# A hybrid encoder layer on one Trainium2 core: w_out's sums, the first pair's operands and half of Norm 2 get new places

## The chip, the core and the metric

The kernel runs on one core of a Trainium2 chip. The core has a matrix engine (TensorE, here PE, with its weight loads PEld), a vector engine (VectorE, DVE), a scalar engine for activations (ScalarE, ACT), a general engine (GpSimd, POOL) and SyncE (SP), which here issues all DMAs. Each works through its own instructions in order and waits on semaphores for the others. Matmuls read the on-chip memory SBUF and write PSUM banks; DVE and ACT empty these. The metric is the device time of one execution in microseconds (us); lower is better.

## The reference

One layer over 2048 rows of width 1024, in fp32. Cut to what matters:

```python
mod  = silu(c) @ w_mod + b_mod                    # 6 vectors: shifts, scales, gates
h    = rms_norm(x, g_norm1) * (1 + scale1) + shift1
qa, ka, va, qm, km, vm, om, gates = split(h @ w_in)
att  = banded_attention(qa, ka, va, sink)         # 8 heads, |t - s| <= 128
mls  = mlstm(conv(qm), conv(km), vm, gates, forward) + mlstm(..., backward)
mix  = concat(rms_norm(att) * g_attn, rms_norm(mls) * g_mlstm * sigmoid(om))
x1   = x + gate1 * (mix @ w_out)
h2   = rms_norm(x1, g_norm2) * (1 + scale2) + shift2
x2   = x1 + gate2 * ((silu(h2 @ w_g) * (h2 @ w_u)) @ w_ffn_out)
out  = rms_norm(x2, g_final)
```

## The kernel before

**Products.** Every fp32 operand is split into a high part (rounded by ACT) and a low part (the rest, by DVE), and one product is three matmuls: high by high, high by low, low by high (`mm3`, L56 to L58). The large products also use a Strassen-like scheme with 7 instead of 8 sub-products on 2 x 2 blocks, for which sums of blocks are formed first.

**Stages**, by the profile's time: up to 192 us modulation, Norm 1 and first projections; to 622 the conv tiles and the mLSTM of four heads, each a reverse pass and a forward pass over 16 chunks of 128 rows; to about 845 attention in 32 units; to 885 the last output gates (`o_tiles`); to 1108 the out projection in eight pairs of row tiles; then the FFN. PE's order is written by hand from the conv stage on: generators in a list `fill` yield one matmul each and `pull(n)` takes n of them in between other work. For the other engines a scheduler sets the order up to the out projection; from `rest` on (L1045) DVE, ACT, POOL and SP work in the order in which the code issues them, until `rest.close()`.

**mLSTM.** For a chunk POOL makes `ng` (L585, decay and mask) and `qs` (L590, scaled queries) from `bc` and `mqk`, which SP loads; ACT takes the exponential of `ng`; PE makes scores `sps`; DVE multiplies them to `sc` (L594); PE adds up `num`. `mv` holds values, `vw` and `kvp` belong to the state.

**w_out's sums.** `w_out_ops` (L855 on) multiplies w_out by the gate and forms the sub-products' seven right operands, on POOL, and stores them to `wo_d`. One group is a block of columns and a k: two loads (`bx`, `by`), multiplications (L871), four differences (L875), seven stores. It advances by `next(wops)` in attention, behind whose units POOL also scales the probabilities `ap` (L695). `start_wo(u)` loads operand u back, `finish_wo(u)` splits it (L892, L893).

**Out projection.** `Pair(p)` loads two tiles of attention's output twice (`msq` to square, `ma` to use), the mLSTM's output `mm` and the output gate `og`. Then: ACT squares, POOL adds (L978, L979), PE sums over partitions (`aps`), DVE takes the root (`rsqrt`) and builds two diagonals, PE spreads them (`arb`), DVE scales (L995) and gates (L998), POOL makes the sums (L1011 to L1020), ACT and DVE split them (L1006, L1007) into the seven left operands. `out_proj` (L1026) runs seven units u of 4 k x 3 matmuls into three PSUM banks. After a unit DVE adds its bank to the rows `xr` of x (L1038), and after units 5 and 6 the rows, now x1, are stored. The loop takes one of 28 steps of a pair with each `pull(1)`, and the next pair's work at fixed steps.

**Norm 2.** `norm2(hh, z, ...)` handles a block of 512 rows: four loads of x1 (`x1t`, L1091), squares (L1100), root, scaling (L1106), PE transposes, ACT's affine (`n`, L163), and for the second block of a half the FFN's sums with the first block's operands, read back from `hop_d`; all operands go to `hop_d`. `refill_ops` loads them (`T`, `B`) and splits them; a FFN unit is `pair(hh, j, ...)`, whose first product is emptied by ACT to `s` (L1302). While pairs 2 and on run, `norm2(0, ...)` is taken a piece every second step; the first FFN unit runs beside pieces of `norm2(1, ...)`.

## Time and profile before

| | us |
|---|---|
| three timed runs, median | 2423.81 |
| lowest and highest | 2422.14, 2426.52 |
| the profiled execution | 2431.26 |
| its span, first to last instruction | 2429.5 |
| PE busy in it | 2271.0 |
| DVE, ACT, POOL busy | 1579.1, 1060.9, 1029.5 |

The profiled execution has its own time, above the timed runs' highest. In the views, each row of instructions names the line, the engine, the operation and the tiles (out <- in); a row of waits names the waiting instruction, then what released it, with the total, the number of times and the longest. "ops" is the PSUM bank of the out projection, "fp" that of a FFN unit, "gps" that of a projection.

### The profile page before, as it was taken

The page shows a single profiled execution, that of the slowest core. Times are in us where ns is not written, and L with a number is a line of the kernel's source. Part 1 is how long each engine was busy: PE and PEld are TensorE (multiplying, and loading weights), DVE is VectorE, ACT ScalarE, POOL GpSimd, SP SyncE. Part 2 cuts the span into 40 slices and gives each one's busy share as a digit, 9 for nine tenths or more (in the row PEclk, how much of TensorE's full clock was granted, in tenths as well). Part 3 has the DMA queues.
Part 4 walks back from the last instruction along what each step waited for, and adds up shares of the span by engine and source line. Part 5 has one row for each costly group of instructions (what it writes and reads, how often), then busy time and mean ns, then how long its engine had stood idle before and what let it go on. Part 6 is the DMA issues. An engine that isn't in the chain of part 4 may idle for free.

```text
span 2429.5 us, 32711 instructions
## 1 busy us (share of the span) xinstructions
PE 2271.0 (93%) x10801; PEld 1876.6 (77%) x10801; DVE 1579.1 (65%) x3096; ACT 1060.9 (44%) x2133; POOL 1029.5 (42%) x874
## 2 busy tenths in 40 slices
PE   5988999999999968888999999999999999999998
PEld 4987777788777856766887887788888888778886
DVE  6774677657677756558655776766566536684584
ACT  4523455544676733426444444543444323223352
POOL 1001234334466333253655565456556546483020
PEclk9999999999999989989999999999999999999999
DMA  7674455576878566685353453533333264453452
GB/s 288 173 239 104 134 164 159 165 214 173 234 239 248 156 212 199 224 282 209 104 169 105 145 178 94 208 91 105 108 111 106 87 212 149 134 173 95 135 200 91
DMA packets 363522, 401.86 MB, mean 165 GB/s; under 512 B 24670, under 2 KB 255576, under 8 KB 363352
## 3 DMA queue, kind: packets, MB, share of 16 engines
q1 hardware_dynamic: 363352, 399.78, 52.0%
q8 instruction: 85, 1.39, 0.2%
q14 instruction: 85, 0.70, 0.1%
HBM read 280.50 MB, written 119.19 MB: 165 GB/s over the span
## 4 chain that ended last, share of the span: by engine, by line
PE 52%; DVE 5%; DMA 4%; issue 2%; ACT 1%; POOL 1%; SPq 1%; DVEq 0%; ACTq 0%; POOLq 0%
PE fp L56 11%; PE fp L58 11%; PE fp L57 11%; PE fo L58 5%; PE fo L57 5%; PE fo L56 5%; PE ops L56 1%; PE ops L57 1%; PE ops L58 1%; DMA hop_d<-n 1%; DMA x1t<-x_d 1%; DMA al<-a_d 1%; PE gps L417 1%; SPq L965 0%; DVE wo L893 0%
## 5 line engine op out<-in xcount | busy, mean ns | idle before, releaser
L417 PE MATMUL gps<-hT,whi 128*128 128x512 f32 x1088 | 400.0, 423 | 12.4 <-ACT ctanh L431 7.3
L56 PE MATMUL fo<-w,ah 128*128 128x512 f32 x616 | 242.6, 394 | 3.0 <-ACT ah L1384 2.9
L58 PE MATMUL fo<-w,al 128*128 128x512 f32 x616 | 243.2, 395 | 1.8 <-DVE al L1385 1.8
L57 PE MATMUL fo<-w,ah 128*128 128x512 f32 x616 | 243.2, 395 | 0.0
L417 PEld LDWEIGHTS gps<-hT,whi 128*128 128x128 f32 x1088 | 203.8, 193 | 38.7 <-ACT ctanh L431 7.7
L417 PE MATMUL gps<-hT,wlo 128*128 128x512 f32 x544 | 229.8, 422 | 0.0
L56 PE MATMUL fp<-T,S 128*128 128x512 f32 x528 | 209.7, 397 | 15.1 <-ACT s L1302 12.5
L58 PE MATMUL fp<-T,S 128*128 128x512 f32 x528 | 208.2, 394 | 0.0
L57 PE MATMUL fp<-T,S 128*128 128x512 f32 x528 | 208.1, 394 | 0.0
L1385 DVE TENSOR_TENSOR al<-al,ah 128x1024 fp32r<-128x1024 f32 x77 | 114.0, 1485 | 137.3 <-ACT ah L1384 137.1
L1186 DVE TENSOR_TENSOR A<-graw,A 128x512 fp32r<-128x512 f32 x86 | 106.3, 1256 | 119.0 <-ACT A L1185 119.0
L1384 ACT ACTIVATE ah<-al 128x1024 fp32r<-128x1024 f32 x77 | 81.7, 1061 | 199.7 <-DMA al<-a_d 197.8
L56 PEld LDWEIGHTS fo<-w,ah 128*128 128x128 f32 x616 | 116.1, 188 | 31.4 <-ACT ah L1384 3.8
L58 PEld LDWEIGHTS fo<-w,al 128*128 128x128 f32 x616 | 115.8, 188 | 29.9 <-DVE al L1385 3.5
L58 PE MATMUL fp<-B,A 128*128 128x512 f32 x352 | 137.6, 391 | 0.0
L56 PE MATMUL fp<-B,A 128*128 128x512 f32 x352 | 137.6, 391 | 0.0
L57 PE MATMUL fp<-B,A 128*128 128x512 f32 x352 | 137.6, 391 | 0.0
L57 PEld LDWEIGHTS fo<-w,ah 128*128 128x128 f32 x616 | 116.0, 188 | 26.7
L56 PEld LDWEIGHTS fp<-T,S 128*128 128x128 f32 x528 | 100.2, 190 | 38.3 <-ACT s L1302 13.4
L1186 DVE TENSOR_TENSOR S<-sf,S 128x512 fp32r<-128x512 f32 x86 | 90.9, 1058 | 44.0 <-ACT S L1185 43.9
L58 PEld LDWEIGHTS fp<-T,S 128*128 128x128 f32 x528 | 99.9, 189 | 22.4
L57 PEld LDWEIGHTS fp<-T,S 128*128 128x128 f32 x528 | 100.2, 190 | 21.7
(376 smaller groups left out, 6067.5 us busy)
## 6 DMA issues: line engine op xcount, KB each, us to landing
al<-a_d SPq DMA_DIRECT2D x77, 512.0 KB, 3.5
wmod<-in_w_mod_dram SPq DMA_DIRECT2D x48, 512.0 KB, 5.8
graw<-in_w_ffn_in_dram SPq DMA_DIRECT2D x43, 512.0 KB, 4.6
a_d<-ka SPq DMA_DIRECT2D x66, 256.0 KB, 2.3
bc<-bc_d SPq DMA_DIRECT2D x64, 256.0 KB, 3.8
hop_d<-n SPq DMA_DIRECT2D x56, 256.0 KB, 4.7
a_d<-u SPq DMA_DIRECT2D x55, 256.0 KB, 3.0
mqk<-qk_d SPq DMA_DIRECT2D x48, 256.0 KB, 4.1
```

The lines of the kernel that those rows point to most:

```text
L56: pe.matmul(o, lh, rh, start=first, stop=False, skip_group_check=skip)
L57: pe.matmul(o, lh, rl, start=False, stop=False, skip_group_check=skip)
L58: pe.matmul(o, ll, rh, start=False, stop=last, skip_group_check=skip)
L417: pe.matmul(ps, w[i == 2][:, k, :], hT[n](i == 1, k), start=(k == 0 and i == 0), stop=(k == KT - 1 and i == 2))
L1186: dve.tensor_tensor(t[:, 1, :], f, t[:, 0, :].bitcast(F32), SUB)
L1384: act.activation(ah, al.bitcast(F32), AF.Copy)
L1385: dve.tensor_tensor(al, al.bitcast(F32), ah.bitcast(F32), SUB)
```

## The change

Five things change.

1. `w_out_ops` moves ahead of the conv and mLSTM loop and is advanced there. It now has four column blocks of 128 instead of two of 256: 16 groups, each with two multiplications of 2 x 128 columns and four differences of 128.
2. A class `Pair` with single steps replaces the old one. Pair 0 goes through its steps in attention (`first_pair`, advanced from unit 21 on) with the first two operands of `wo`.
3. In the loop over pairs, loads come three pairs ahead, attention's output is loaded once, high splits (HI) and low splits (LO) are separate steps, and `xr` has five buffers.
4. For the first half of T, Norm 2 is done from the rows `xr` on chip, pair by pair, by the class `Rows`; its root is taken together with the next pair's. Its 128x512 tiles `n2` have nine buffers. The second half keeps `norm2`, now all on DVE.
5. In the last pair and the first FFN unit, the other engines' order is written out (`then=first_unit`), and `rest` closes behind that unit. `norm2(1, ...)` starts in the second unit. Rings of buffers are turned.

POOL's order in head 0, where the reverse pass ends; `wlo` is the low part of a conv weight, `ng` and `qs` belong to the scan. Before:

```order
L585 TENSOR_TENSOR ng<-bc,maskb 128x256 x2
L231 TENSOR_TENSOR wlo<-wraw,whi 128x1024
L590 TENSOR_TENSOR qs<-mqk,bc 128x256 x2
L231 TENSOR_TENSOR wlo<-wraw,whi 128x1024
L585 TENSOR_TENSOR ng<-bc,maskb 128x256 x2
```

Now, the last two of the groups that stand between `ng` and `qs`:

```order
L832 TENSOR_TENSOR bx<-bx,gb 128x256
L836 TENSOR_TENSOR ts<-bx 128x128
L832 TENSOR_TENSOR by<-by,gb 128x256
L836 TENSOR_TENSOR ts<-by,bx 128x128
L836 TENSOR_TENSOR ts<-by,ts 128x128 x2
L234 TENSOR_TENSOR wlo<-wraw,whi 128x1024
L832 TENSOR_TENSOR bx<-bx,gb 128x256
L836 TENSOR_TENSOR ts<-bx 128x128
L597 TENSOR_TENSOR qs<-mqk,bc 128x256 x2
```

Five groups, and the start of a sixth, have come ahead of the first `qs`.

SP's order at the same place, where the third `mv` of the reverse pass and the first `mqk` of the forward pass are loaded. Before:

```order
L433 DMA qk_d<-cacc 128x512 x3
L503 DMA mv<-vaug_d 128x4x129
L508 DMA mqk<-qk_d 128x512
L522 DMA bc<-bc_d 128x512
L503 DMA mv<-vaug_d 128x4x129
```

Now, first where `mv` stands, then, four rows further, where `mqk` stands:

```order
L436 DMA qk_d<-cacc 128x512
L839 DMA wo_d<-bx 128x128
L510 DMA mv<-vaug_d 128x4x129
L839 DMA wo_d<-by 128x128 x2
L839 DMA wo_d<-ts 128x128
L840 DMA wo_d<-ts 128x3x128
L824 DMA gb<-gate_d 128x128 x2
```

```order
L839 DMA wo_d<-bx 128x128
L839 DMA wo_d<-by 128x128 x2
L839 DMA wo_d<-ts 128x128
L840 DMA wo_d<-ts 128x3x128
L828 DMA bx<-in_w_out_dram 128x2x128
L515 DMA mqk<-qk_d 128x512
L828 DMA by<-in_w_out_dram 128x2x128
```

`mv` now stands behind the fourth group's first store, `mqk` behind the fifth group's stores.

POOL's order at the end of pair 3 and the start of pair 4 (`n` are the `n2` tiles of Norm 2, `ms` and `mm` the pair's sums, `msq` the next pair's squares). Now:

```order
L971 TENSOR_TENSOR mm<-mm,ms_11258 128x512
L1200 TENSOR_TENSOR n_11391<-n_11373,n_11360 128x512
L1203 TENSOR_TENSOR n_11322<-n_11322,n_11320 128x512
L1200 TENSOR_TENSOR n_11434<-n_11412,n_11399 128x512
L1203 TENSOR_TENSOR n_11326<-n_11326,n_11324 128x512
L941 TENSOR_TENSOR msq<-msq 128x256
L942 TENSOR_TENSOR msq<-msq 128x128
L941 TENSOR_TENSOR msq<-msq 128x256
L942 TENSOR_TENSOR msq<-msq 128x128
```

The second L1200 writes the buffer of `n_11373` (B22 of the first half), so it waits for that tile's store. Before, the pairs had only this between them:

```order
L1011 TENSOR_TENSOR ma<-ma 128x512
L1012 TENSOR_TENSOR ms_10887<-mm,ma 128x512
L1017 TENSOR_TENSOR ma<-ms_10887,ma 128x512
L1020 TENSOR_TENSOR mm<-mm,ms_10887 128x512
L978 TENSOR_TENSOR msq<-msq 128x2x256
L979 TENSOR_TENSOR msq<-msq 128x2x128
```

The Norm 2 sums of the first half have come in ahead of the squares' sums.

The diff, cut to its core:

```diff
@@ ahead of the conv and mLSTM loop (before: in front of attention) @@
+    wqs = ExitStack()
+    wq = wqs.enter_context(tc.tile_pool(name="wq", bufs=1, side="left", reuse_waits="tile"))
+    def w_out_ops():
-        for c_ in range(2):
-            cs = slice(c_ * 256, (c_ + 1) * 256)
+        for c_ in range(4):
+            cs = slice(c_ * P, (c_ + 1) * P)
+            gb = cp.tile([P, 2, P], F32, tag="gn", name="gb", bufs=1)
...
             for k in range(4):
+                bx, by = (wq.tile([P, 2, P], F32, tag=t, name=t) for t in ("bx", "by"))
+                for t, k_ in ((bx, k), (by, k + 4)):
+                    sp.dma_start(t, w_out[k_ * P:(k_ + 1) * P].rearrange("p (m c) -> p m c", m=2)[:, :, cs])
+                yield True
+                ts = wp.tile([P, 4, P], F32, tag="oth", name="ts", bufs=1)
+                for t in (bx, by):
+                    pool.tensor_tensor(t, t, gb, MUL)
+                    yield True
...
+                for u, t in ((0, bx[:, 0, :]), (1, by[:, 0, :]), (5, by[:, 1, :]), (6, ts[:, 3, :])):
+                    sp.dma_start(wo_d[u, k][:, cs], t)
+                sp.dma_start(wo_d[2:5, k, :, cs].rearrange("u p c -> p u c"), ts[:, 0:3, :])
+                yield True
@@ conv and mLSTM loop @@
     for h in range(HM):
-        for g in convs[h]:
-            finish_fill(g)
+        i = 0
+        while any(f is g for f in fill for g in convs[h]):
+            pull(1)
+            i += 1
+            if i % 2 == 0:
+                next(wops, None)
         last = load_last(h)
-        pull(60)
+        for i in range(60):
+            pull(1)
+            if i % 2 == 0:
+                next(wops, None)
         mlstm(h, 3, 8, last)
@@ class Pair @@
+        def square(self, i, sq):
+            act.activation(sq, self.a[:, i], AF.Square)
+            pool.tensor_tensor(sq[:, 0:2], sq[:, 0:2], sq[:, 2:4], ADD)
+            pool.tensor_tensor(sq[:, 0], sq[:, 0], sq[:, 1], ADD)
...
+        def hi(self):
+            u = len(self.ops)
+            self.f = (self.a11, self.a12, self.s2, self.a11, self.a21, self.a12, self.a22)[u]
+            self.ops.append(mring_tile(("mA11", "mA12", "mS2", "mS1", "mS3", "mS4", "mA22")[u]))
+            act.activation(self.ops[u][:, 0, :], self.f, AF.Copy)
+        def lo(self):
+            t = self.ops[-1]
+            dve.tensor_tensor(t[:, 1, :], self.f, t[:, 0, :].bitcast(F32), SUB)
@@ attention @@
-            if s_ > 4:
-                next(wops, None)
-        if not wo and s_ > 31 and lasts[0] not in fill:
-            for u in range(2):
-                start_wo(u)
+        if s_ > 20:
+            next(chain0, None)
@@ class Rows @@
+        def turn(self, k):
+            t = self.new()
+            ps = bank("bd"[self.n % 2], "trn")
...
+            for j in range(4):
+                pe.transpose(ps[:, j * P:(j + 1) * P], self.xr[j % 2][:, (k + j // 2) * P:(k + j // 2 + 1) * P], ident)
+            for j in range(2):
+                act.activation(t[:, j * 256:j * 256 + 256], ps[:, j * 256:j * 256 + 256], AF.Identity,
+                               bias=mod[:, 3, k + j:k + j + 1], scale=gs2[:, k + j:k + j + 1])
+            return t
+        def step(self, i):
...
+            g = 2 * (i > 20)
+            if i in (17, 21):
+                self.b12 = self.turn(g)
+            if i in (18, 22):
+                self.b22 = self.turn(g + 4)
+            if i in (20, 24):
+                b11, b12, b22 = self.t[g], self.b12, self.b22
+                self.t3 = self.new()
+                pool.tensor_tensor(self.t3, b22, b12, SUB)
+                dve.tensor_tensor(b12, b12, b11, SUB)
+                dve.tensor_tensor(b11, b22, b12, SUB)
+                pool.tensor_tensor(self.t[g + 1], self.t[g + 1], b11, SUB)
+                self.done = [("B22", g, b22), ("T3", g, self.t3), ("T1", g, b12), ("T2", g, b11), ("T4", g, self.t[g + 1])]
+            if i in (23, 27):
+                for o in self.done:
+                    self.put(*o)
@@ loop over pairs @@
-    OPERANDS = (5, 7, 10, 13, 16, 19, 23)
-    FIRST = (1, 2, 5, 8, 10, 14, 18)
+    HI, LO = (5, 8, 10, 14, 16, 19, 22), (6, 9, 11, 15, 17, 20, 23)
+    FIRST = (1, 2, 5, 8, 16, 20, 24)
...
-        if p in (2, 4):
-            norms.append(norm2(0, p // 2 - 1, "bd", 3))
...
+            if i == 18:
+                nx3 = Pair(p + 3) if p + 3 < NPR else None
+                if nx3:
+                    nx3.load_a()
...
+                if i == 7:
+                    ps = bank("a", "aps")
+                    for j in range(2):
+                        columns(ps, j, sq[j])
+                if i == 8:
+                    parts = [(ps[:, :2], 2, 512)] + ([(prev.ssq, 2, D)] if prev else [])
+                    r = rsqrt(mx, parts, 2 * len(parts), None, f"ar{len(parts)}")
...
+                prev.step(i)
+            if p < 4 and i == 25:
+                rows = Rows(p, xr0)
+                rows.square(0)
@@ FFN @@
+        def first_unit(u):
+            nonlocal nxt_w
             if u < 3:
                 finish_op(u + 4)
+            for _ in range((0, 0, 1, 1, 2, 1, 2)[u]):
+                nxt_w = next(more_w)
...
+            elif n == 0:
+                more_w = weights(raw)
+                pair(hh, j, ws_, hop, then=first_unit)
+                rest.close()
+                raw = load_raw(wseq.popleft())
```

397 lines of the change are left out of this document (227 added, 170 removed).

## The prediction

> **What bounds the kernel now.** I read the page's head first, then busy time by stage, then what TensorE (PE) waited for, and last the engines behind those waits. The profiled execution took 2431.3 us (span 2429.5, and 1.8 around it); the median of the three timed runs is 2423.8, so 7.4 us or 0.3% less. I sum against 2431.3 and take the 7.4 off at the end.
>
> ```profile
> span 2429.5 us, 32711 instructions
> PE 2271.0 (93%) x10801; PEld 1876.6 (77%) x10801; DVE 1579.1 (65%) x3096; ACT 1060.9 (44%) x2133; POOL 1029.5 (42%) x874
> ```
>
> PE is busy 93% of the span, so time can only go where PE stands still or runs slowly. The table by stage says where (columns: PE, weight loads, DVE, ACT and POOL busy with instruction counts, the clock granted to PE, the DMA engines' share):
>
> ```profile
> 885.00:920.00 35.00, 23.30 (x91) 18.10 (x91) 31.68 (x46) 17.18 (x23) 10.54 (x6) 0.85 0.38 120
> 920.00:974.00 54.00, 43.69 (x190) 35.20 (x189) 33.17 (x80) 19.36 (x29) 18.68 (x12) 0.94 0.61 200
> 974.00:1029.00 55.00, 46.76 (x221) 38.21 (x219) 32.04 (x79) 24.29 (x37) 17.12 (x12) 0.94 0.70 230
> 1029.00:1088.00 59.00, 47.91 (x206) 38.53 (x205) 34.92 (x60) 16.42 (x25) 31.47 (x21) 0.88 0.83 280
> 1088.00:1108.00 20.00, 20.00 (x90) 16.41 (x89) 14.84 (x20) 12.69 (x17) 1.30 (x1) 1.00 0.94 352
> 1108.00:1139.00 31.00, 22.26 (x86) 17.67 (x85) 25.25 (x34) 20.78 (x31) 12.94 (x9) 0.83 0.49 165
> 1139.00:1400.00 261.00, 256.33 (x1135) 209.43 (x1134) 159.11 (x180) 114.78 (x194) 151.00 (x104) 0.99 0.40 129
> ```
>
> From 885 to 1139 us run the out projection (eight pairs of row tiles) and the first FFN unit: 254 us. Only the pair at 1088 runs without a break; elsewhere PE is idle for 15 to 33%, and the clock is reduced too. From 1139 on it is 2%. The rows give 884 matmuls; 9 x 84 = 756 of them are the 128x512 products, which start 0.23 us apart at full clock (below): 172 us. The other 128 are short, about 5 us by their number. So about 77 us of the 254 are lost. What PE waited for from 868 on (the fourth row is one wait in front of the stage, at 873):
>
> ```profile
> PE ops L56 <- DVE xr L1038: 29.7, 8, 7.8
> PE fp L56 <- ACT s L1302: 8.7, 1, 8.7
> PE trn L162 <- ACT n L163: 5.4, 2, 5.0
> PE gps L417 <- ACT oth L489: 5.1, 1, 5.1
> PE ops L56 <- ACT mA L1006: 4.8, 1, 4.8
> PE aps L985 <- POOL msq L979: 3.7, 2, 2.3
> ```
>
> (Columns: total, times, longest.) The five rows of the stage make 52 us, so about 25 of the 77 are slow clock and short pauses; with the 5.1 in front 82 are lost. A matmul of the next unit waits until VectorE (DVE) has emptied its PSUM bank, and DVE works in written order behind low-half splits that wait for ScalarE (ACT). ACT in turn:
>
> ```profile
> ACT n L163 <- DMA hop_d<-n: 26.8, 5, 11.7
> ACT junk L1100 <- DMA x1t<-x_d: 16.2, 2, 8.2
> DMA to landing us min/median/max: 7.1/7.7/8.3
> ```
>
> So Norm 2's reload of x1 (`x1t`; the third row is its landing, 7.7 us in the median) holds ACT, ACT holds DVE, DVE holds PE. A stall also costs something behind itself:
>
> ```profile
> 1073.18 0.79 PE L56 MATMUL ops<-wo,mS 128*128 128x512 f32 x1 [3.07 <-DVE xr L1038]
> 1073.77 0.63 PE L57 MATMUL ops<-wo,mS 128*128 128x512 f32 x1
> 1074.20 0.63 PE L58 MATMUL ops<-wo,mS 128*128 128x512 f32 x1
> ...
> 1076.88 0.40 PE L56 MATMUL ops<-wo,mS 128*128 128x512 f32 x1
> 1077.11 0.40 PE L57 MATMUL ops<-wo,mS 128*128 128x512 f32 x1
> ```
>
> After a wait of 3.07 us the matmuls start 0.43 us apart until about 1076.5, then 0.23: some 1.7 us more. The Trainium skill, TensorE: Matmul & The Clock Gate, section "HAM oscillation — how this bites in real kernels", gives the rule that PE must not idle for more than about 3.4 us; here 3.07 us were enough, and the measurement decides. By the page's limit the new waits below, which I put at 3.5 us, would be at its edge and the sum could be 3 us smaller; by the row they pay.
>
> **Part 1, out projection and first FFN unit: 82 us lost, 28 left, gain 54.** For the first half of T Norm 2 now squares the rows that are still on chip; eight x1t loads go, and with them the two ACT waits (16.2 us), and the hop reads in front of `n` come ten steps ahead of use. Operands are loaded three pairs ahead; high and low splits are separate steps, so DVE no longer stands behind a split that waits for ACT. Work per pair stays: DVE has 7 adds, 7 low splits, 4 scalings and a gate in each pair:
>
> ```profile
> L1038 DVE TENSOR_TENSOR xr<-xr,ops 128x512 f32<-128x512 f32 x56 | 38.1, 681 | 18.3 <-PE ops L58 18.3
> L1007 DVE TENSOR_TENSOR mA<-mm,mA 128x512 fp32r<-128x512 f32 x15 | 15.1, 1006 | 4.6 <-ACT mA L1006 4.6
> L995 DVE SCALAR_TENSOR_TENSOR ma<-ma,cols,arb 128x256 f32<-128x256 f32 x28 | 11.6, 474 | 5.4 <-PE arb L993 5.4
> L998 DVE SCALAR_TENSOR_TENSOR mm<-og,mm 128x1024 f32<-128x1024 f32 x7 | 8.5, 1216 | 0.0
> L1123 POOL TENSOR_TENSOR n<-n,n 128x512 f32<-128x512 f32 x4 | 5.1, 1286 | 5.3 <-DMA hop_d<-n 5.3
> ```
>
> 7 x 0.68 + 7 x 1.0 + 4 x 0.47 + 1.2 = 14.9 us, and some 3 for the root, against 19.3 us (84 x 0.23) of PE: it fits, so a pair's stalls can go. Two pairs get four sums of Norm 2 on DVE as well (no row shows them there; below the 1.29 of POOL's row each), up to 23: these two are tight. What I leave: 5 us of the entry into pair 0 (pair 0's operands now come out of attention, but the low splits of `wo` still stand in DVE's order), 6 in pairs 1 to 3, 4 in pairs 6 and 7, 3 in the first FFN unit, whose 8.7 us wait goes because no Norm 2 of the second block stands in it. Nothing measures these; bounds are 0 and 29: the 5.1, 4.8, 5.4 and 3.7 above, 19 us, with 1.7 of slow clock for each of the six.
>
> And one **new wait**, 10 us. Pairs 3 and 4 write five results per half and the nine `n2` buffers go round. POOL's second T3 writes the buffer of the first B22, whose store to hop_d is issued only behind unit 5's x1 store, and lands late:
>
> ```profile
> hop_d<-n SPq DMA_DIRECT2D x56, 256.0 KB, 4.7
> ```
>
> So POOL stands from step 24 to about 5 us later. Behind it on POOL: its 1.3 us, the T4 sum 1.3, then the next pair's sums of squares (2.4), which PE needs at step 7: 10.0 us of work in 11 steps x 0.68 = 7.5, some with DVE's sum in between, whose queue holds the PSUM adds. About 3.5 us of PE and 1.5 of slow clock, twice: 10. Bounds 0 (if the store lands in 2 us) and 20.
>
> **Part 2, attention: gain 7.** The 64 POOL instructions and the loads they wait for leave:
>
> ```profile
> L871 POOL TENSOR_TENSOR bx<-bx,gb 128x256 f32<-128x256 f32 x16 | 11.6, 736 | 25.9 <-DMA bx<-in_w_out_dram 25.6 <-DMA by<-in_w_out_dram 0.3
> PE atp L702 <- POOL ap L695: 8.6, 18, 3.4
> ```
>
> 64 x 0.74 = 47 us of POOL and 25.6 of waiting stood in `ap`'s queue, and PE waited 8.6 us for `ap`, one time long enough for the slow clock (some 2 us). Pair 0's loads, squares, root, scaling and gate come in instead, a few us over 13 steps: 10.6 less 3.6. Bounds 0 and 12.
>
> **Part 3, mLSTM: loss 16.** The same sums now come as 16 groups in 128-wide pieces beside the conv and the scans: 2 multiplications of 0.74 us and 4 differences at about 0.46 (an estimate: 0.74 for 256 wide and 1.29 for 512 differ by 0.55), 3.3 us a group. bx and by have one buffer each, so a cycle is: load (4.0, row below), 3.3, two stores to issue (0.8): about 8.1 us. In head 0's reverse pass five such cycles stand in POOL's and SP's order. SP reaches the load of the gate only after the store of the conv in the second row, and the mLSTM's own loads are queued behind the cycles:
>
> ```profile
> DMA to landing us min/median/max: 3.5/4.0/4.3
> 239.45 6.05 SPq L433 DMA_DIRECT2D qk_d<-cacc  x2
> 262.71 0.37 SPq L503 DMA_DIRECT2D mv<-vaug_d  x1
> 263.65 0.93 SPq L508 DMA_DIRECT2D mqk<-qk_d  x1
> 279.09 0.38 PE L592 MATMUL sps<-mqk 128*128 128x128 f32 x1 [1.61 <-DVE cb L565]
> ```
>
> The gate lands at about 243.5. The third `mv`, behind the fourth group's first store, is issued at 243.5 + 3 x 8.1 + 0.7 = 268.5 instead of 262.7; the forward pass's first `mqk`, behind the fifth group's stores, at 243.5 + 4 x 8.1 + 4.6 = 280.5 instead of 263.7, and it lands about 284.5. PE needs it at 279.1: 5.4, say 6 us. In the forward passes POOL's `ng` has a slack:
>
> ```profile
> 280.31 0.73 POOL L585 TENSOR_TENSOR ng<-bc,maskb 128x256 f32<-128x256 f32 x1 [3.20 <-DVE sc L594]
> 284.58 0.42 DVE L594 SCALAR_TENSOR_TENSOR sc<-sps,ng 128x256 f32<-128x256 f32 x1
> L104 DVE TENSOR_TENSOR mra<-mra,mrh x48: 148/161/2159, 298.7 to 608.2; 128x4 f32<-128x4 f32 x48
> ```
>
> from 281.0 to 284.6, less two ACT steps: about 2.7 us. A half group puts 1.2 to 2.1 us ahead of an `ng`, and up to 4 of waiting for a load. Seven groups, 14 halves, 0.7 us each beyond the slack: 10. Bounds of part 3: 0 (all within slack) and 14 x 2 + 12 = 40.
>
> **Sum:** -54 - 7 + 16 = -45; 2431.3 - 45 = 2386.3, and less 7.4: **2379 us**.
>
> **Rivals.** (a) *The entry and the new wait are hidden.* For it: in pair 1088 to 1108 PE shows no idle time though DVE was 74% busy. Then 10 + 5 + 3 us more go: 2361. (b) *The new wait runs on.* DVE's queue behind POOL makes the next pairs start late too, and five of them pay 7 us (the longest wait at `xr` is 7.8 now) in place of 10 in all: 25 us more, 2404. For it: DVE and POOL are coupled there now too (the 5.3 us in the T3 row), against it: pairs 5 to 7 store nothing to hop_d. (c) *The change doesn't do what it says:* the x1t loads go but the waits under "xr L1038" come from DVE's own order, so half of the 29.7 and of the 25 us of slow clock stays: 27 us back, 2406. Against it is the chain shown above. (d) *Slower: the mLSTM pays more than the rest gains.* POOL is one queue; if a group's whole 8.1 us cycle lies on PE's path, the gain of 61 is gone after 7.5 of the 16 groups, that is, once half of them land in the scans without slack; with nine it is 73: 2424 - 61 + 73 = 2436. For it: half of the groups do stand in the two heads' passes. Against it: only the part beyond 2.7 us counts. The `mra` row feeds it: a tiny DVE instruction of 0.16 us took 2.16 beside one of POOL's. The Trainium skill, GPSIMD Engine Reference, section "1. Specifications", says that POOL's SBUF interfaces are shared with VectorE and that instructions with two SBUF inputs contend; the trace agrees with that 2.16 us. By that rule each of the 96 instructions could hold DVE for its own length, at most 53 us on top.
>
> **How the numbers follow.** Forecast as summed 0.56; (a) 0.12; (b) 0.13; (c) 0.08; (d) 0.07; and 0.04 for an mLSTM loss that just eats the gain. A measurement of this kernel tells about 0.2% (5 us) from no change. Faster: 0.89, within: 0.04, slower: 0.07. The range reaches from (a)'s with 10 us of the bounds, 2351, past (b) and (c) to 2412, and leaves out (d).
>
> **What would show it.** Right: no `x1t` in the first half, `ops <- xr` under 12 us, no wait over 3 us in the first FFN unit, and a wait at `aps` in the pairs behind 3 and 4 with POOL behind hop_d. The mLSTM's end moves from 622 to about 638 and its loads `mv` and `mqk` go out late. Wrong: if the mLSTM ends at 625 or at 660; if PE waits in pair 0 as before; or if POOL never stands for hop_d.

## The result, and the profile after

| | before | after |
|---|---|---|
| timed runs, median, us | 2423.14 (4 runs, 2422.14 to 2426.52) | 2407.76 (4 runs, 2406.51 to 2408.81) |
| ratio, with 95% interval | | 0.9934 [0.9917, 0.9951] |
| profiled execution, us | 2431.26 | 2408.62 |

The change makes the kernel 15.4 us faster between the medians, 0.66% by the ratio. The forecast was 2379: 28.8 us too low, inside its range of 2351 to 2412. Between the two profiled executions the gain is 22.6 us, where the sum said 45. The head of the page of after:

```profile
span 2406.8 us, 32761 instructions
PE 2275.5 (95%) x10801; PEld 1889.9 (79%) x10801; DVE 1587.8 (66%) x3078; ACT 1062.4 (44%) x2157; POOL 1032.1 (43%) x922
```

Both kernels have 10801 matmuls, and but for a stretch from 750 to 1066 us, in which short ones have moved, in the same order, so the k-th matmul of one can be set against the k-th of the other. (At 873 after has four products of the gates fewer behind it and four short matmuls more, about 0.9 us.) The table gives after's start less before's, worked out from the two traces: a falling number is time gained, a rising one time lost.

| matmul that starts in before at | shift, us | what lies between |
|---|---|---|
| 240 (first groups of w_out begin in after) | -2.7 | not touched by the change |
| 279 (first `sps` of head 0's forward pass) | +5.5 | reverse pass of head 0 |
| 300, 360, 400 | +11.2, +23.5, +30.2 | heads 0 and 1 |
| 622 (first attention score) | +32.7 | rest of head 1, heads 2 and 3: the mLSTM lost **35.4** in all |
| 873 | +18.4 | attention gained **14.3** |
| 1108 (first FFN unit starts) | -18.3 | entry and eight pairs gained **36.7** |
| 1139 (second unit starts) | -29.3 | first unit gained **11.0** |
| 1152 | -18.5 | second unit gave **10.8** back |
| 2400 | -22.5 | little |

So after is 4.0 us better in the FFN and 2.7 us ahead before the change begins. Both are of the size by which executions of one kernel differ (single runs of before on the chips lay between 2417.7 and 2431.3). The table by stage of after shows the same from PE's side (columns as in the prediction; stages cut where the same matmuls stand):

```profile
899.00:930.00 31.00, 23.47 (x90) 18.37 (x89) 28.62 (x45) 16.39 (x25) 9.72 (x8) 0.83 0.42 134
930.00:968.00 38.00, 38.00 (x188) 31.58 (x187) 30.27 (x65) 22.15 (x38) 17.58 (x16) 1.00 0.61 199
...
1090.00:1109.50 19.50, 19.15 (x84) 15.29 (x83) 18.53 (x17) 12.75 (x19) 7.91 (x4) 1.00 0.83 302
1109.50:1133.50 24.00, 17.29 (x58) 13.15 (x57) 18.11 (x30) 14.59 (x23) 11.93 (x8) 0.82 0.36 110
```

Pairs 1 and 2 (second row) and the first unit (third row) now run almost without a break; the entry (first row) keeps 7.5 us of idle time, and the pairs that the dots leave out keep 5.9. Behind the first unit stands a stretch that was not there in before: 24 us with PE idle for 6.7 of them and its clock at 0.82. What PE waited for from 870 to 1140, first, and the heaviest waits of the mLSTM stage of after, second (columns: total, times, longest):

```profile
PE aps L989 <- POOL msq L942: 10.8, 8, 2.7
PE fp L56 <- ACT u L1460: 4.6, 2, 4.2
PE ops L56 <- DVE xr L1090: 4.2, 2, 3.5
PE fp L56 <- ACT s L1452: 2.5, 1, 2.5
...
PE sps L599 <- DVE sc L601: 16.3, 9, 3.7
PE kvp L548 <- DVE den L629: 6.8, 2, 5.0
PE ktp L538 <- ACT og L648: 5.1, 1, 5.1
PE sps L599 <- DMA mqk<-qk_d: 4.8, 1, 4.8
```

The same view of before, from 240 to 622, has none of these long ones:

```profile
PE sps L592 <- DVE sc L594: 7.6, 8, 1.8
PE kvp L541 <- DVE den L622: 3.6, 2, 2.1
```

`xr` fell from 29.7 to 4.2, as forecast. In the mLSTM waits of 3.7 to 5.1 us are new. They are not the whole loss. The same matmuls as a stage, before and after:

```profile
240.00:622.00 382.00, 359.25 (x2021) 303.00 (x2019) 260.52 (x909) 183.82 (x563) 136.77 (x156) 0.99 0.59 169
```

```profile
237.50:654.70 417.20, 371.56 (x2020) 313.62 (x2019) 268.99 (x909) 182.87 (x563) 188.82 (x252) 0.95 0.64 184
```

Of the 35 us, 23 are idle time of PE (22.8 to 45.6), and 12 are its busy time, which grew while the granted clock fell from 0.99 to 0.95: the matmuls run slowly here too. SP's issues in head 0's reverse pass of after show where the first of them come from (start, duration, transfer):

```profile
266.56 0.43 SPq L510 DMA_DIRECT2D mv<-vaug_d  x1
...
277.56 0.42 SPq L840 DMA_DIRECT2D wo_d<-ts  x1
...
278.72 0.55 SPq L515 DMA_DIRECT2D mqk<-qk_d  x1
```

`mv` goes out at 266.6 (forecast 268.5, before 262.7), `mqk` at 278.7 (forecast 280.5, before 263.7): SP stands at w_out's stores until POOL has made their data. POOL in turn waits for the loads in front of them (busy, mean ns; then idle time in front and what ended it):

```profile
L832 POOL TENSOR_TENSOR bx<-bx,gb 128x256 f32<-128x256 f32 x16 | 12.4, 777 | 54.1 <-DMA bx<-in_w_out_dram 47.7 <-DMA gb<-gate_d 6.1 <-DMA bc<-bc_d 0.3
```

### The profile page after: what moved, and what is told of

The parts are those of the page before. It is cut to its first block, busy times and chain, and to the rows that moved or that the text cites. A ratio compares the mean times of both kernels' runs of the same rounds, so it can differ in the third digit from the quotient of the medians.

```text
span 2406.8 us, 32761 instructions
## 1 busy us (share of the span) xinstructions
PE 2275.5 (95%) x10801; PEld 1889.9 (79%) x10801; DVE 1587.8 (66%) x3078; ACT 1062.4 (44%) x2157; POOL 1032.1 (43%) x922
## 4 chain that ended last, share of the span: by engine, by line
PE 72%; DVE 8%; DMA 8%; issue 4%; POOL 3%; ACT 3%; SPq 1%; POOLq 0%; ACTq 0%; DVEq 0%
PE fp L56 11%; PE fp L57 11%; PE fp L58 11%; PE gps L420 8%; PE fo L58 6%; PE fo L56 6%; PE fo L57 5%; PE ops L56 2%; PE ops L57 2%; PE ops L58 2%; DMA bc<-bc_d 1%; PE atp L709 1%; DMA vst_d<-vs 1%; DVE macc L336 1%; PE as L686 1%
## 5 line engine op out<-in xcount | busy, mean ns | idle before, releaser
L420 PEld LDWEIGHTS gps<-hT,whi 128*128 128x128 f32 x1088 | 205.8, 195 | 30.8 <-ACT ctanh L434 5.0
L56 PEld LDWEIGHTS fp<-T,S 128*128 128x128 f32 x528 | 101.1, 191 | 37.3 <-ACT u L1460 8.2
L702 POOL TENSOR_SCALAR ap<-ap,adn 128x384 f32<-128x384 f32 (+1 forms) x128 | 72.9, 588 | 130.9 <-DVE adn L700 57.2
L58 PEld LDWEIGHTS fp<-T,S 128*128 128x128 f32 x528 | 101.0, 191 | 22.8
```

The lines of the kernel that those rows point to most:

```text
L56: pe.matmul(o, lh, rh, start=first, stop=False, skip_group_check=skip)
L58: pe.matmul(o, ll, rh, start=False, stop=last, skip_group_check=skip)
L420: pe.matmul(ps, w[i == 2][:, k, :], hT[n](i == 1, k), start=(k == 0 and i == 0), stop=(k == KT - 1 and i == 2))
L702: pool.tensor_scalar(self.p[g][:, :self.NK], self.p[g][:, :self.NK], dn[:, g:g + 1], 0.0, MUL, ADD)
```

## The experiments

In every run the mLSTM's loss is measured in one way: the shift against before at matmul 622 less that at 240. All times of single runs are one profiled execution. Up to the out projection POOL, VectorE and ACT have the same instructions in the same order in after, f_skip, f_step, f_pool and o_noput, so these five show how far one and the same code differs from execution to execution: the mLSTM lost 34.0 to 38.6 us in them, and attention gained 9.7 to 15.2. A difference under 5 us between two runs of the table shows nothing.

| run | shift at 240 | at 622 | mLSTM lost | time, us |
|---|---|---|---|---|
| after | -2.7 | +32.7 | 35.4 | 2408.6 |
| m_none | +6.7 | +7.4 | 0.7 | 2384.9 |
| m_nopool | +3.7 | +8.4 | 4.7 | 2387.3 |
| m_noload | -1.8 | +19.6 | 21.4 | 2397.9 |
| m_spread | +1.3 | +38.6 | 37.3 | 2411.7 (median) |
| m_poolq | -3.7 | +73.3 | 77.0 | 2449.2 |
| m_db | -0.5 | +26.8 | 27.3 | 2400.8 |
| m_poolonly | +6.7 | +45.9 | 39.2 | 2421.2 |
| m_late | -3.6 | +17.3 | 20.9 | 2396.3 |
| b_late | -0.3 | +21.6 | 21.9 | 2394.0 (median) |
| b_spread | -0.1 | +21.6 | 21.7 | 2392.1 (median) |
| b_paced | -2.5 | +29.5 | 32.0 | 2402.3 (median) |
| b_paced3 | -3.3 | +32.5 | 35.8 | 2405.7 (median) |

### What of w_out's work costs the mLSTM its 35 us

**m_none** (no w_out work beside the mLSTM):

```diff
-        for c_ in range(4):
-            ...
+        for _ in range(128):
+            yield True
...
+        if s_ < 14:
+            for k in (0, 2):
+                sp.dma_start(wo_d[s_ // 2, k + s_ % 2], w_out[k * P:(k + 1) * P, 0:512])
```

> Leaves out w_out's multiplications, differences, loads and stores beside the mLSTM; wo_d is filled with raw columns of w_out by copies from memory to memory during attention, so the out projection multiplies by other numbers. Everything else is the changed kernel. It prices the move: in the changed kernel PE's first attention score starts at 654.7 us, before the change at 622.1. If the groups of w_out are what the mLSTM lost its 35 us to, the first score starts at 618 to 623 us here. If something else in the change holds the mLSTM (buffers, another order of SP), it stays above 640.

**m_noload** (the loads of all groups but the first are left out):

```diff
-                bx, by = (wq.tile([P, 2, P], F32, tag=t, name=t) for t in ("bx", "by"))
+                if k == 0 and c_ == 0:
+                    bx, by = (wq.tile([P, 2, P], F32, tag=t, name=t) for t in ("bx", "by"))
...
+                    if k == 0 and c_ == 0:
+                        sp.dma_start(t, w_out[k_ * P:(k_ + 1) * P].rearrange("p (m c) -> p m c", m=2)[:, :, cs])
```

> Leaves out the loads of bx and by for all groups but the first, so w_out's operands are wrong; POOL's 96 instructions and all stores stay. Theory QUEUE (POOL and SP stand in order behind each group's loads, with one buffer each, and the mLSTM's own loads and its ng and qs stand behind them): most of the 35 us goes, first attention score at 632 us or before (changed kernel 654.7). Theory WORK (POOL's 53 us of instructions take its time and hold VectorE beside them): little goes, 645 us or later.

**m_nopool** (POOL's instructions are left out; loads and stores stay):

```diff
                 for t in (bx, by):
-                    pool.tensor_tensor(t, t, gb, MUL)
                     yield True
...
-                    pool.tensor_tensor(ts[:, z, :], f, g, SUB)
                     yield True
```

> Leaves out the two multiplications and four differences of each group; loads and stores stay, and the stores send what was loaded. QUEUE: POOL has nothing of w_out to wait with, but SP still waits for each load before its stores and for the stores before the next load, with mv and mqk behind: between 630 and 645 us for the first attention score. WORK: nearly all goes, 628 us or before.

**m_spread** (one step for each chunk of the scans, in place of every second pull):

```diff
         for cc in list(range(NT - 1, 0, -1)) + [0, 0]:
             tick()
+            next(wops, None)
...
         for cc in range(NT + 1):
             tick()
+            next(wops, None)
```

> All of the work is done, and one step of w_out's groups is taken in each chunk of the mLSTM's passes in all four heads (136 steps) in place of every second matmul of the conv in heads 0 and 1. QUEUE: a group has eight chunks for its cycle of some 8 us, so cycles no longer pile up; loss of the mLSTM under 15 us (first score 632 to 640 us) and the kernel at 2385 to 2395 us. WORK: the same 53 us of POOL work, loss stays 25 to 35 us, 2400 to 2410 us.

*Measured.* Without any w_out work 0.7 us is lost, so the 35 are all of its making. (The first score came at 629.4, above the 618 to 623 expected: this execution was 6.7 us late before the groups' place already, which no run explains.) Without POOL's instructions 4.7 are lost, though every load and store is still there (one store of each group as two); without the loads 21.4. By their first scores, 630.5 is in QUEUE's range and 641.7 between the two theories. m_spread changed nothing (37.3; ratio to before 0.9936 [0.9918, 0.9954]), nearest to WORK. So the price hangs on POOL's instructions, and on what waits for them, far more than on the DMAs themselves. It was open whether that is their own time, or SP standing for them.

### SP's order, or POOL's time

**m_poolq** (w_out's DMAs issued by POOL): `sp.dma_start` becomes `pool.dma_start` in the five places of `w_out_ops`.

> After with all of w_out's loads and stores of the mLSTM stage issued by GpSimd's own queue in place of SyncE's; the work is the same. Measure: how far the first attention score lies behind that of before, less the shift at 240 us; after lost 35 us there, of that all but 5 go when GpSimd's instructions are left out. Theory ORDER (SyncE stands for GpSimd's results in its order, and the mLSTM's own loads mv and mqk wait behind those stores): SyncE has nothing left to stand for, mv and mqk go out as in before (within 2 us of 262.7 and 263.7 plus the shift at 240), and the loss falls to 5 to 18 us, of which the issuing on GpSimd takes what stays. Theory CONTENTION (GpSimd's instructions themselves slow or hold VectorE and the mLSTM's own GpSimd steps): the same instructions stand there, so the loss stays at 30 us or more, though mv and mqk are early.

*Measured:* 77.0 us lost, against both theories. SP's `mv` and `mqk` did go out early (259.9 and 260.8), but POOL paid for each issue:

```profile
L839 POOL DMA_DIRECT2D wo_d<-by x32 | 18.5, 577 | 0.0
L840 POOL DMA_DIRECT2D wo_d<-ts x16 | 12.2, 762 | 0.0
```

0.54 to 0.76 us an issue, about as long as a multiplication: some 4.5 us more for a group of seven DMAs, on the queue that also makes `ng` and `qs`. The run can't tell the theories apart, but it shows that POOL's queue is on PE's path there.

**m_db** (two buffers):

```diff
-                bx, by = (wq.tile([P, 2, P], F32, tag=t, name=t) for t in ("bx", "by"))
+                bx, by = (wq.tile([P, 2, P], F32, tag=t, name=t, bufs=2) for t in ("bx", "by"))
```

> After with two buffers each for bx and by in place of one; ts has one as before. Theory ORDER: the loads may go out a group earlier, but SyncE's stores still wait for GpSimd in SyncE's order; the wait at bx shrinks from 54 us to below 25, and the loss in the mLSTM falls only in part, to 20 to 30 us. Theory LOAD WAITS (the prediction's: the cycle of 8.1 us is set by the load of 4.0 that can't start before the store): a cycle falls to some 4.5 us, the loss falls to 10 to 17 us. Theory CONTENTION: no change, 33 to 38 us.

*Measured:* 27.3, inside what ORDER said. POOL's idle time in front of `bx` fell from 54.1 to 19.0 us, but another wait came in: the differences' tile `ts` kept one buffer, and POOL now waits for its store:

```profile
L836 POOL TENSOR_TENSOR ts<-bx 128x128 f32<-128x128 f32 x16 | 7.5, 467 | 27.0 <-DMA wo_d<-ts 26.7
```

In after the idle time in front of that line is 0.9. So second buffers for `bx` and `by` alone are worth 8 us; what the cycle of load and store costs as a whole this run doesn't show.

**m_poolonly** (only POOL's 96 instructions stay): the edits of m_noload, the stores left out, and the copies of m_none.

> After with only GpSimd's 96 instructions of w_out left beside the mLSTM: bx and by are loaded once, no group is stored there, and the 28 products' operands in wo_d are filled by copies within DRAM during attention, so w_out's operands hold other numbers. Loss in the mLSTM as in the other runs (first attention score, less the shift at 240 us): 35 us in after, 21 with the loads left out, 5 with GpSimd's instructions left out. Theory ORDER (SyncE stands for GpSimd's results with the mLSTM's loads behind it): with no store to stand for, the loss falls to 0 to 10 us. Theory CONTENTION (GpSimd's instructions themselves push the mLSTM's own GpSimd steps and slow VectorE): it stays at 18 us or more.

*Measured:* 39.2 lost, which looks like CONTENTION. The trace says otherwise. SP's issues there:

```profile
278.80 15.54 SPq L824 DMA_DIRECT2D gb<-gate_d  x4
294.38 0.43 SPq L436 DMA_DIRECT2D qk_d<-cacc  x1
294.91 0.38 SPq L510 DMA_DIRECT2D mv<-vaug_d  x1
```

With the loads gone, POOL's order was another, and SP came to loads of `gb`, which has one buffer. It stood there until POOL had read the gate before, and `mv` behind it went out at 294.9 in place of 262.7. The loss is whole at 279 already (36.6 us), and over the 343 us to 622 the shift moves by 2.6. So the run tests neither theory as it was meant to, since another wait took the store's place; but SP standing for POOL with the mLSTM's loads behind it is shown more plainly than by any other run.

**m_late** (two buffers, and a group's stores behind the next group's loads):

```diff
+                yield True
+                while late:
+                    sp.dma_start(*late.pop(0))
                 ts = wp.tile([P, 4, P], F32, tag="oth", name="ts", bufs=1)
...
-                    sp.dma_start(wo_d[u, k][:, cs], t)
-                sp.dma_start(wo_d[2:5, k, :, cs].rearrange("u p c -> p u c"), ts[:, 0:3, :])
+                    late.append((wo_d[u, k][:, cs], t))
+                late.append((wo_d[2:5, k, :, cs].rearrange("u p c -> p u c"), ts[:, 0:3, :]))
```

> After with two buffers each for bx and by, and each group's stores issued behind the next group's loads, two steps later, so that GpSimd has mostly finished when SyncE comes to them; the work is all done. After lost 35 us in the mLSTM, with the two buffers alone 27. ORDER: most of the rest goes, loss 8 to 18 us, and mv and mqk of head 0's forward pass go out within 5 us of before's. CONTENTION: 24 to 30 us, no better than the two buffers alone.

*Measured:* 20.9, between the two; `mv` and `mqk` go out at 267.4 and 267.9, within 5 us of before. 14.5 of the 35.4 (12 to 18 by the spread of that code) are thus single buffers of `bx` and `by` and early stores. POOL still stands 28.1 us here for the store of `ts`, which has one buffer as in m_db; no run gave it a second. A part of the rest is still SP's order: its store of head 0's output and ACT's next use of that buffer,

```profile
369.97 0.57 SPq L649 DMA_DIRECT2D mxm_d<-og  x1
```

```profile
374.72 0.69 ACT L648 ACTIVATE og<-htp,gml 128x512 f32<-128x512 f32 x1 [8.06 <-DMA mxm_d<-og]
```

show it: ACT waited 8.1 us for the buffer that SP was late to empty, with w_out's transfers ahead of that store, and PE then waits 7.5 us at `ktp` behind ACT.

**b_late** is m_late with B22's store moved (below). **b_spread** is b_late with the steps of m_spread.

> The change with the two edits that earlier runs point to: bx and by with two buffers and the stores of a group behind the next group's loads (that run took 11.5 us less than after's profiled one), and B22 of the first half stored as soon as the half is done, in place of three steps later, so that GpSimd's second T3 finds its buffer free. All work is done. If the late store is the wait (storing other numbers there took 7.5 us off between 944 and 1089), both waits at aps go and the run comes to 2385 to 2393 us, 1.3 to 1.6% under before; if an earlier issue isn't enough, the waits stay over 1.5 us each and it stays at 2393 to 2399.

> As the run above, and w_out's steps are taken one per chunk of the mLSTM's scans, over all four heads, in place of every second pull of the first two heads. Open: whether the 21 us that the mLSTM still lost with late stores come from SyncE standing at w_out's DMAs in a dense stretch (ORDER), or from GpSimd's 96 instructions wherever they stand among the scans (CONTENTION). ORDER: spread out, each store finds its data ready, the mLSTM loses 3 to 12 us and the run is 8 to 18 us below the run above. CONTENTION: the loss stays at 17 to 25 us and the run is within 4 us of it. With single buffers and early stores the same spreading had changed nothing (37 for 35).

*Measured:* b_late 2393.97 (5 runs; ratio 0.9877 [0.9857, 0.9896]), b_spread 2392.14 (4 runs; 0.9858 [0.9841, 0.9876]); in the mLSTM 21.9 and 21.7. (b_late's median is 1 us above the 2385 to 2393 expected.) By the expectation the second is CONTENTION, but the spreading had not taken place: the multiplications of b_late, first, and of b_spread, second (last figures: first and last start):

```profile
L836 POOL TENSOR_TENSOR bx<-bx,gb x16: 722/732/742, 243.9 to 375.0; 128x256 f32<-128x256 f32 x16
```

```profile
L838 POOL TENSOR_TENSOR bx<-bx,gb x16: 724/737/743, 244.1 to 372.7; 128x256 f32<-128x256 f32 x16
```

POOL's order is the scheduler's, and by these starts it hardly moved with the place where the code issues the work. m_spread had been as good as void for the same reason (245 to 426, after 241 to 419).

**b_paced** ties each group to the scans; **b_paced3** then takes two differences in a step, so that the groups end with the third head:

```diff
+                if mark:
+                    zc = wq.tile([P, 1], F32, tag="zc", name="zc")
+                    pool.tensor_tensor(zc, mark[0], zz, MUL)
+                    pool.tensor_tensor(bx[:, 0, 0:1], bx[:, 0, 0:1], zc, ADD)
                 for t in (bx, by):
                     pool.tensor_tensor(t, t, gb, MUL)
```

(`zz` is zero, `mark` the newest chunk's `kn` or `hst`.)

> As b_spread (late stores, two buffers, early store of B22), and now tied to the scans: the scheduling layer had not kept the steps apart (w_out's multiplications ran from 244 to 373 us in b_spread, 244 to 375 in b_late), so neither run had spread anything. Here each group first takes in a zero made from the newest chunk of the scan on GpSimd (two instructions on one column), so it can't start before that chunk, and the 16 groups go four to each head. All work is done. ORDER or density: the mLSTM loses 3 to 12 us in place of 22, and the run is 8 to 18 us below b_spread. CONTENTION (96 instructions and the waits in front of them cost what they cost wherever they stand): the loss stays at 17 to 25 us. If GpSimd's new waits for the scan are dearer than what they save, it is above 25.

> As b_paced, with two differences to a step, so that the 16 groups end with the third head. In b_paced the mLSTM had lost only 6.4 us up to 450 us of before (11 of the groups done; b_late had lost 20.5 there with all 16), and 25 more between 450 and 600, where SyncE also issues the stores of attention's keys and queries and runs without a break. Theory QUEUE (a group costs little where neither SyncE nor GpSimd is made to stand; the last five groups cost what they did because SyncE was full there): the loss at 622 is 6 to 14 us and the run 8 to 16 us below b_spread (2392), that is 2376 to 2384. Rival (the denser pace costs in heads 0 to 2 what it saves in head 3): loss 18 us or more, the run no better than b_spread.

*Measured:* the groups did spread (242 to 580 us, and 241 to 514), and it got worse than b_late: 32.0 and 35.8 lost, 2402.33 us (0.9913 [0.9895, 0.9931]) and 2405.68 us (0.9927 [0.991, 0.9944]). In b_paced only 6.4 us were lost up to 450 and 25.6 in the two heads behind it; the reading that SP was full there fell with b_paced3, which lost all of its 35.8 in the first three heads. Part of it is the tie's own price:

```profile
L847 POOL TENSOR_TENSOR zc<-kn,zz 128x1 f32<-128x1 f32 x9 | 1.7, 189 | 29.1 <-ACT kn L543 29.1
```

POOL idled 29.1 us in front of nine such instructions, so these runs show that wide spacing is no cure, and not what POOL's instructions cost by themselves.

### The second FFN unit

**f_skip** takes Norm 2's pieces out of the second unit (`beside if n > 1 else lambda u: None`).

> After without Norm 2's pieces for the second half of the rows beside the second FFN unit; they begin in the third, so fewer units are left for them, and all of them are still taken. In after the stretch from the first matmul of the second FFN unit (1109.5) to where the next phase is even with before again (1152) takes 42.9 us where before's takes 31.4. Theory N2 (VectorE and GpSimd are full with Norm 2's pieces, weight splits stand behind them): the stretch falls to 31 to 36 us, the run by 5 to 11 us, if the pieces cost nothing later. Theory DEBT (the splits of the second unit's weights come late because they were pushed out of the first): the stretch stays above 40 us and the run within 3 us of after.

**f_step** makes the third unit's operands beside the second unit's products (`pair(hh, j, ws_, hop, beside, steps)` with one or two pieces of `weights` per product) in place of ahead of them.

> After with the weights of the third FFN unit turned into operands step by step beside the products of the second (as the first unit does for the second) in place of all at its head; the fourth unit's raw weights are loaded behind that. All work is done. In after the stretch from 1109.5 (second unit) to 1152 takes 11 us more than before, and leaving Norm 2's pieces out of it changed nothing. Theory DEBT (the splits of late weights stand ahead of the unit's own ACT and VectorE steps): the waits at fp of 2.5 and 4.2 us in the second unit go and its stretch falls by 6 to 11 us; if the debt is only handed on, a wait of 4 us or more turns up in the third unit (from 1133 on) and the run is within 4 us of after. Rival (GpSimd's and VectorE's own work in the second unit is too much whatever its order): the second unit stays as slow, within 3 us.

**f_pool** makes three of seven low halves on POOL, for the second and third unit's weights:

```diff
-            dve.tensor_tensor(t[:, 1, :], f, t[:, 0, :].bitcast(F32), SUB)
+            (pool if n in low else dve).tensor_tensor(t[:, 1, :], f, t[:, 0, :].bitcast(F32), SUB)
```

> After with three of the seven low-half differences of the weights of the second and third FFN unit (S1, S3, A22) made by GpSimd in place of VectorE. VectorE is busy without a break from 1085 to 1112 there, and the third unit's raw weights are loaded only when the second's last differences have read their buffers (1114.5). Theory DVE (VectorE's work in the first unit is the bound, a wait of before had given it the time): the third unit's loads go out 2 us or more earlier against the first unit's start, and the second unit loses 4 to 9 us against before in place of 11. Rival (what counts is the length of the chain of loads and sums, and GpSimd at 1.3 us an instruction and sharing with VectorE is no faster): 10 to 14 us lost, loads no earlier.

The columns are times of before, in which the second unit starts at 1138.6 and the third at 1157.9. (The expectations' 1109.5 and 1152 are times of after.)

| run | shift at 1108 | at 1139 | at 1152 | at 1200 |
|---|---|---|---|---|
| after | -18.3 | -29.3 | -18.5 | -17.8 |
| b_late | -37.2 | -48.1 | -36.8 | -35.3 |
| f_skip | -14.0 | -25.0 | -14.9 | -14.0 |
| f_step | -15.0 | -25.9 | -21.0 | -14.3 |
| f_pool | -8.4 | -19.4 | -8.1 | -2.0 |

*Measured* (one execution each: 2411.6, 2414.7 and 2424.1 us; after's 2408.6). f_skip: nothing, so Norm 2's pieces are not it. f_step: 6 us of the stall went (the wait of 4.2 us at `u` is 0.4), and came back by 1200 in waits of 2.4 and 2.1 us at `c`. The wait of 2.5 us at `s` stayed. That is a debt handed on, though in shorter waits than the 4 us expected. f_pool: no gain, and 6 us lost behind it. Its loads came no earlier (24.9 us behind the first unit's first matmul; 25.1 in after). Most of its longer time, 9.9 us, stands ahead of the first unit, where its edit hasn't begun.

Except in f_step, **the shift at 1152 is that at 1108 within 1 us**, and so it is in all the other runs but one (m_nopool, 2.3 us), wherever the stages in front had put the first unit. That these runs agree among themselves says only that the FFN, which most of them leave alone, does not depend on what stands ahead of it. That before takes the same 44 us is more, but no proof of a chain that PE doesn't set: in before PE waits for nothing in the second unit, and ACT waits for PE there. What the traces show is the path of the weights. SP's issues in after:

```profile
1093.00 0.39 SPq L1293 DMA_DIRECT2D graw<-in_w_ffn_in_dram  x1
...
1114.53 0.38 SPq L1294 DMA_DIRECT2D A<-in_w_ffn_in_dram  x1
```

and in before:

```profile
1109.96 0.83 SPq L1172 DMA_DIRECT2D graw<-in_w_ffn_in_dram  x1
...
1129.52 0.37 SPq L1173 DMA_DIRECT2D A<-in_w_ffn_in_dram  x1
```

Raw weights have one buffer, loaded again once the splits have read it. The second unit's are asked for 3.6 us behind the first unit's first matmul (1089.4), the third's 25.1 us behind it (in before 2.2 and 21.8 behind 1107.7). ACT ends the last of the third unit's high splits 38.6 us behind that first matmul in after (1128.0) and 37.2 in before (1144.9): a first unit that is 11 us shorter doesn't bring these weights forward. In after these splits stand in ACT's order ahead of the second unit's own `t` and `u`, and PE waits for `u`:

```profile
1127.41 0.63 ACT L1306 ACTIVATE S<-graw 128x512 fp32r<-128x512 f32 x1 [1.12 <-POOL graw L1318]
1127.94 0.61 ACT L1456 ACTIVATE t<-g 128x512 f32<-128x512 f32 x1
1128.46 0.58 ACT L1460 ACTIVATE u<-fp 128x512 f32<-128x512 f32 x1
```

```profile
1129.09 0.79 PE L56 MATMUL fp<-T,S 128*128 128x512 f32 x1 [4.20 <-ACT u L1460]
```

In before PE lost the same time in the first unit, which took 31 us, and the weights were ready by the second. f_step shows the place in ACT's order to be the wait at `u`; that the weights' path as a whole is what holds the second unit is argued from these rows. Which link sets its length (the landing of the loads, POOL's sums, or the buffer) no run here singles out.

### The new wait at hop_d

**o_noput** stores T4's tile in B22's place in the first half:

```diff
-                self.done = [("B22", g, b22), ("T3", g, self.t3), ...
+                self.done = [("B22", g, b22 if i == 24 else self.t[g + 1]), ("T3", g, self.t3), ...
```

> After, but in the two pairs that keep results in hop_d the first half stores T4's tile in the place of B22's, so that part of hop_d holds other numbers and the buffer that GpSimd's second T3 takes is not waited for behind a store. In after TensorE waits 3.0 us (1004) and 2.2 us (1033) at aps in the pairs behind these two. Theory of the prediction (the late store of B22 holds GpSimd): both waits go, and the run is 5 to 8 us shorter (the waits and some slow clock). Rival (GpSimd's sums are late for VectorE's and TensorE's own pace, or another store of the nine buffers holds it in turn): both stay within 1 us of that, and the run within 2 us of after.

**b_late** has, for the same, `self.put("B22", g, b22)` at the half itself, three steps earlier, and all stores are right. In after POOL stood as forecast (the second T3, then the T4 sum and the squares' sums that PE needs):

```profile
997.83 1.29 POOL L1200 TENSOR_TENSOR n<-n,n 128x512 f32<-128x512 f32 x1 [3.03 <-DMA hop_d<-n]
1000.72 1.29 POOL L1203 TENSOR_TENSOR n<-n,n 128x512 f32<-128x512 f32 x1 [1.60 <-DVE n L1202]
1001.97 1.71 POOL L941 TENSOR_TENSOR msq<-msq 128x256 f32<-128x256 f32 x1
```

and in b_late it doesn't:

```profile
983.34 1.75 POOL L1206 TENSOR_TENSOR n<-n,n 128x512 f32<-128x512 f32 x1
```

*Measured:* between 944 and 1089 of before, after gains 23.4 us (+5.1 to -18.3), o_noput 30.9 (+4.0 to -26.9) and b_late 30.9 (-6.3 to -37.2). The two waits at `aps`, each in two parts (2.18 and 0.83 us at 1004, 2.24 and 0.63 at 1033), are 0.7 us each in both. An earlier issue is enough. The other runs tell how sure the price is: all eleven others that keep the late store gain 23.4 to 25.6 there, the three b_ runs besides b_late 30.8. So the late store cost 5.2 to 7.5 us.

Not tried: w_out's sums in attention as before, beside the first pair's operands, since there is no room for their buffers; and more than nine `n2` buffers, for the same reason.

## Why the prediction was off

The forecast was a gain of 45 us by the sum, and 22.6 came between the two profiled executions. Two of its steps failed, the second term of part 3 and the end of part 1. By its own steps, against the profiled execution:

- **Part 3, mLSTM: 16 forecast, 35.4 measured; this step failed by its size.** Head 0's reverse pass was right in kind: `mv` and `mqk` went out within 2 us of the forecast, a group's cycle took 8.0 us (its first multiplications from 241.5 to 281.5 in five steps) for 8.1, and the shift to 279 was 8.2 us for the 6 forecast. The second term, "14 halves, 0.7 us each beyond the slack: 10", measured 27. It priced one thing that lies behind a group, POOL's `ng`. The runs show that a group holds SP as well, and with it each of the scan's loads and stores (`mv`, `mqk`, the store of `og`): mending buffers and store order alone takes 14 us off. It also had no term for slow clock, which parts 1 and 2 had, and 12 of the 35 us are busy time at a lower clock. Of the other 21, 16 go only when POOL's instructions go (m_nopool against m_late, 4.7 and 20.9, which differ in more than that). How much of that is their place in the queue, how much is POOL standing for the store of `ts` (28.1 us in m_late), and how much is slower VectorE beside them is open. The last is the small part as far as VectorE's own busy time tells: it grew by 8.5 us in after (260.5 to 269.0, rows above) and by 5.6 in m_late.
- **Part 1: 54 forecast to the end of the first unit; 47.7 measured there (+18.4 to -29.3), but 36.9 at 1152.** The step that failed is "3 in the first FFN unit, whose 8.7 us wait goes because no Norm 2 of the second block stands in it". The wait did go, and the first unit ran at full pace. But it had covered the time until the weights of the units behind it were ready: the third unit's are split 37 to 39 us behind the first unit's start in either kernel, so PE's 11 us were given back in the second unit, which the sum didn't hold. The prediction asked nowhere what is late next there.
- **The new wait: 10 forecast, 5.2 to 7.5 measured,** at the place and by the store named. The waits themselves were 3.0 and 2.9 us for 3.5 twice. The entry into pair 0 kept waits of 2.7 and 3.5 us, for the 5 left to it.
- **Part 2, attention: 7 forecast, 14.3 measured** (9.7 to 15.2 over the five executions of this code), mostly outside its bounds of 0 to 12, which came from PE's waits at `ap` alone. The stage before, and after:

```profile
622.00:870.00 248.00, 235.47 (x1236) 195.82 (x1236) 182.94 (x507) 169.11 (x438) 132.69 (x200) 0.99 0.76 231
```

```profile
654.70:891.50 236.80, 228.27 (x1235) 193.66 (x1236) 183.93 (x522) 170.36 (x444) 91.95 (x143) 0.99 0.64 190
```

  PE's idle time fell by 4.0 us (12.5 to 8.5; its waits at `ap` alone by 7.0, from 8.6 to 1.6), near the forecast, and its busy time by 7.2 for nearly the same matmuls (five of the gates' products fewer, about 1.2 us). 4.7 of that lie in the 368 transposes of `ap` (61.2 to 56.5). For the busy time the sum had no term, and no run looked for its cause.
- **The 7.4 us between before's profile and its median did not carry over.** After's profiled execution is 0.9 above its median. Before's was simply a long one: 6.5 us of the miss.

Together: 19.4 (part 3) + 17.1 (part 1, the new wait in it) - 7.3 (part 2) - 6.7 (stages that the change leaves alone) = 22.5 us between the traces, and 6.5 of the conversion make the 28.8, but for rounding.

Of the rivals, (d) named the mechanism that decided, with POOL's queue and SP's behind it, but at 73 us twice what it cost. (b) didn't happen: the new wait stays with two pairs. Neither did (c): no `x1t` is loaded before 1097.8. (a) didn't happen either: the entry and the new wait cost what is said above, and its first unit at full pace came true and gained nothing.

The clock rule that the prediction weighed fell further short. After a wait of 2.52 us, with no other pause near it, the matmuls start up to 0.43 us apart too, until about 1121.5:

```profile
1117.49 0.50 PE L56 MATMUL fp<-T,S 128*128 128x512 f32 x1 [2.52 <-ACT s L1452]
...
1119.01 0.63 PE L57 MATMUL fp<-T,S 128*128 128x512 f32 x1
1119.44 0.63 PE L58 MATMUL fp<-T,S 128*128 128x512 f32 x1
```

The Trainium skill, TensorE: Matmul & The Clock Gate, section "HAM oscillation — how this bites in real kernels", puts the limit of an idle gap at about 3.4 us; by it this wait would have cost its length alone. Ten matmuls behind it took 4.0 us where ten at 0.23 take 2.3.

The faster version that the runs point to is b_spread or b_late, which can't be told apart: 1.2 to 1.4% below before, where after is 0.7%.

## What to carry to other kernels

A wait that is taken away must be followed to the next link: where a unit starts earlier, ask whether its successors' data, which the old wait covered, are ready; equal shifts at both ends of a stretch, in variants that leave the stretch alone, don't yet show what sets its length. Work that is put "beside" another stage is priced on every in-order queue that it passes through, the DMA queue above all: a store that waits for its data holds all loads behind it, so it is issued when the data are there, and loads get a second buffer; a second buffer for some of the tiles can move the wait to the one that has none (`ts` in m_db). And before a variant is read as evidence, look in its trace whether the edit moved what it was meant to move; two of these had hardly done so.

## What the runs showed of the hardware that was not expected

POOL's instructions with two inputs and VectorE's slow each other at the large sizes too. In after VectorE's low split of 128x512 takes 0.66 to 0.70 us in all 290 cases in which no two-input instruction of POOL overlaps it in time, and 1.3 in the median, 1.81 at most, in the 280 in which one does, as in the second row. POOL's sum of 128x512 takes at most 1.30 where no two-input instruction of VectorE overlaps it (45 cases), and up to 2.37 where one does. (VectorE's first row is two of 1.22 elsewhere.)

```profile
1101.73 4.46 DVE L1267 TENSOR_TENSOR T<-T,T 128x1024 fp32r<-128x1024 f32 x2
1106.12 1.78 DVE L1307 TENSOR_TENSOR A<-graw,A 128x512 fp32r<-128x512 f32 x1
```

```profile
1102.95 2.16 POOL L1312 TENSOR_TENSOR sf<-sf,graw 128x512 f32<-128x512 f32 x1
```

A DMA issued by POOL holds POOL for 0.54 to 0.76 us (m_poolq), longer than the 128x128 difference (0.46 to 0.52) whose result it stores.

And the length of the slow clock behind a wait jumps. PE's wait at `xr` in pair 0 stands in the traces of after and of all its variants. In the eleven in which it lasted 3.09 to 3.54 us, the matmuls behind it were slow for 2.7 to 3.3 us; in the six in which it lasted 3.58 to 3.71, for 5.7. Why, no run here shows.
